# A part of the low-part subtractions goes from VectorE to GpSimd

## The chip, the cores and the metric

The kernel runs on one core of one Trainium2 chip. The metric is the device time of one execution in microseconds; the median of several executions is compared.

## The reference

The program takes one sequence of 256 tokens of width 1024, in float32, through two blocks of two layers each.

The first block has a hybrid layer (a gated linear recurrence with a short convolution beside retention), a feed-forward layer `(silu(x @ w1) * (x @ w3)) @ w2` with 2816 hidden columns, a sparse-attention layer (compressed, selected and windowed keys; at 256 tokens all four selection blocks are taken), and a second feed-forward layer, each behind an RMS norm and with a residual sum. The second block has two layers of four branches (full attention, windowed attention with a sink, a Fourier mix, a spatial gate), each with a gated merge; they work on the tokens and, in the first of them, on a context of 256 more tokens, and their norms are modulated by vectors made from two condition vectors and the matrices `w_ada`.

Nearly all the time goes into matrix products of the 256 tokens with weights of 1024 rows. The result has to hold float32 accuracy.

## The kernel before

TensorE multiplies in the type `float32r`. To keep accuracy, each operand is split into a high part (the value rounded to that type by a ScalarE copy) and a low part (the value less its high part), and each product is three matmuls: low by high, high by low, high by high (`mm3`, L420, L421, L422, the first operand being the stationary one).

Weights lie in three lists in memory, cut into pieces of 128 x 1024 in the order in which they are used: `wmain` (object `w_x`, all that the tokens' layers need), `wctx` (`w_c`, the context's projections) and `wada` (`w_a`, the modulation's matrices). A piece comes in through one of four `raw` buffers by a DMA on SyncE's queue (`load`, L316). `Weights.parts` then makes its two parts: ScalarE copies `raw` to the high part `whi` (L339), VectorE subtracts to get the low part `wlo` (L340), both into one of three pairs of buffers or into a big buffer with another name (M, B, C). The raw buffer is free for the next load when both have read it. `w_x` makes one piece ahead of the one asked for (`ahead` 1). `k` counts the pieces made. The list `los` holds the subtractions, and `behind` uses it to keep some VectorE instructions (L811 in the group norm, L1127 in the query and key norm) behind the next subtraction in VectorE's order.

The order of the instructions on each engine comes from the framework's scheduler, which works from the program's order, from what is ready by its own estimates, and from a few orders written out with `tc.issue_after`. Each engine then works through its instructions in order.

The stages that the change touches:

- The hybrid layer takes 32 pieces: four each for q, xr, k, v, g and y, eight for the output. Its group norm takes a power on GpSimd (L475) between VectorE instructions (L474, L811).
- The residual sum (L614) and the norm before the first feed-forward layer follow: squares on ScalarE, small VectorE instructions (L485, L486), a power on GpSimd (L487), a scaled copy on VectorE (L493), transposes on TensorE (L511).
- The first feed-forward layer (`ffn`) has 22 blocks. Block j takes two up pieces, applies the gate, and splits the result (tile `fp`); from block 2 on one down piece follows each time, for the block two before (`Out.step`). Before each block `hook(j)` runs: it moves the modulation on by two steps (`first`), and from block 8 on the context layer by two (`side_by`). A modulation step loads one piece of `wada` into a raw buffer and adds it, scaled, to two sums on VectorE (L1089 for the first, L1091 for the others); 18 steps make two modulation vectors, and so they end with block 8.
- The third stage (`nsa`) projects, then runs 16 units of attention; in each the context moves on by one step.

GpSimd does only powers of a few columns and some fills.

## Time and profile before

| | |
|---|---|
| median of three runs | 1454.93 us (1454.76 to 1458.89) |
| profiled execution | 1458.04 us, its span 1456.3 us |
| TensorE busy | 1402.7 us, 96% of the span |
| VectorE busy | 962.7 us, 66% |
| ScalarE busy | 710.2 us, 49% |
| GpSimd busy | 38.6 us, 3% |
| mean granted TensorE clock | 0.984 |

The span runs from the first to the last instruction of the profiled execution. Matmuls are pipelined and their ends are modelled, so that a busy TensorE is not TensorE at its peak. In the rows PE is TensorE, DVE is VectorE, ACT is ScalarE, POOL is GpSimd and SPq is SyncE's queue of DMA issues.

### The profile page before, as it was taken

How to read it: one execution, taken by the hardware profiler on the slowest of the kernel's cores; microseconds unless marked ns; L12 is line 12 of the kernel's file. 1: busy time of each engine (PE TensorE's matmuls, PEld its weight loads, DVE VectorE, ACT ScalarE, POOL GpSimd, SP SyncE). 2: the span in 40 equal slices, each digit the busy share in tenths (PEclk: the TensorE clock that was granted, in tenths of full speed). 3: DMA queues.
4: the chain of work that ended last, by engine and by line, in shares of the span. 5: the costliest groups of instructions: out<-in, count | busy, mean ns of one | idle time of the engine just before them, and what ended most of it. 6: DMA issues, size and time to landing. Idle time of an engine off the chain costs nothing.

```text
span 1456.3 us, 24385 instructions
## 1 busy us (share of the span) xinstructions
PE 1402.7 (96%) x9815; PEld 1265.0 (87%) x9815; DVE 962.7 (66%) x1675; ACT 710.2 (49%) x1203; POOL 38.6 (3%) x46
## 2 busy tenths in 40 slices
PE   7998999999899999999999999999999999999998
PEld 6887889988697678989888798999999878889997
DVE  7967886645676677768776776354443677665566
ACT  5743446456455664444445575333332345654453
POOL 0010000000000000000000100000000011100000
PEclk9999999999998999999999999999999999999999
DMA  8645777546353026677775553233333516413663
GB/s 295 210 126 189 259 254 234 181 138 196 97 151 117 1 63 211 212 238 231 229 259 178 155 159 89 72 117 103 116 117 116 159 64 184 151 53 109 187 181 124
DMA packets 65745, 230.31 MB, mean 158 GB/s; under 512 B 7776, under 2 KB 9312, under 8 KB 65376
## 3 DMA queue, kind: packets, MB, share of 16 engines
q1 hardware_dynamic: 65632, 228.76, 49.9%
q8 instruction: 77, 1.26, 0.4%
q14 instruction: 36, 0.29, 0.1%
HBM read 227.68 MB, written 1.05 MB: 157 GB/s over the span
## 4 chain that ended last, share of the span: by engine, by line
PE 76%; DVE 9%; DMA 6%; ACT 5%; issue 3%; POOL 1%; SPq 0%; ACTq 0%; DVEq 0%; POOLq 0%
PE P L420 12%; PE P L421 12%; PE P L422 12%; PE Q L420 6%; PE Q L422 6%; PE Q L421 6%; PE R L420 4%; PE R L421 4%; PE R L422 4%; DVE wlo L340 3%; DMA raw<-in_wmain_dram 3%; PE P L431 3%; DMA raw<-in_wada_dram 2%; PE R L428 2%; PE Q L431 2%
## 5 line engine op out<-in xcount | busy, mean ns | idle before, releaser
L340 DVE TENSOR_TENSOR wlo<-raw,whi 128x1024 fp32r<-128x1024 f32 (+2 forms) x325 | 392.1, 1209 | 195.7 <-ACT whi L339 194.1
L339 ACT ACTIVATE whi<-raw 128x1024 fp32r<-128x1024 f32 (+2 forms) x325 | 340.3, 1048 | 323.6 <-PE P L422 80.2
L420 PE MATMUL P<-B,wlo 128*128 128x256 f32 x752 | 216.2, 287 | 0.0
L422 PE MATMUL P<-B,whi 128*128 128x256 f32 x752 | 213.7, 284 | 0.0
L421 PE MATMUL P<-B,whi 128*128 128x256 f32 x752 | 213.4, 284 | 0.0
L420 PE MATMUL Q<-B,wlo 128*128 128x256 f32 x704 | 202.7, 288 | 3.4 <-DVE wlo L340 2.4
L422 PE MATMUL Q<-B,whi 128*128 128x256 f32 x704 | 200.6, 285 | 0.0
L421 PE MATMUL Q<-B,whi 128*128 128x256 f32 x704 | 200.2, 284 | 0.0
L420 PEld LDWEIGHTS P<-B,wlo 128*128 128x128 f32 x752 | 143.8, 191 | 3.0 <-issue 1.4
L421 PEld LDWEIGHTS P<-B,whi 128*128 128x128 f32 x752 | 143.8, 191 | 0.7 <-issue 0.3
L422 PEld LDWEIGHTS P<-B,whi 128*128 128x128 f32 x752 | 143.8, 191 | 0.4 <-issue 0.2
L420 PEld LDWEIGHTS Q<-B,wlo 128*128 128x128 f32 x704 | 135.9, 193 | 7.8 <-DVE wlo L340 4.0
L421 PEld LDWEIGHTS Q<-B,whi 128*128 128x128 f32 x704 | 136.0, 193 | 1.3
L422 PEld LDWEIGHTS Q<-B,whi 128*128 128x128 f32 x704 | 135.9, 193 | 0.3 <-issue 0.2
L420 PE MATMUL P<-whi,B 128*128 128x512 f32 (+3 forms) x264 | 101.4, 387 | 5.3 <-DVE B L411 5.3
L421 PE MATMUL P<-wlo,B 128*128 128x512 f32 (+3 forms) x264 | 99.0, 376 | 0.5 <-DVE wlo L340 0.5
L422 PE MATMUL P<-whi,B 128*128 128x512 f32 (+3 forms) x264 | 98.9, 375 | 0.0
L1091 DVE SCALAR_TENSOR_TENSOR M<-raw,silu_c,M 128x1024 f32<-128x1024 f32 x42 | 53.8, 1281 | 36.9 <-DMA raw<-in_wada_dram 36.8
L420 PE MATMUL R<-C,wlo 128*128 128x256 f32 x272 | 76.3, 280 | 0.0
L421 PE MATMUL R<-C,whi 128*128 128x256 f32 x272 | 76.0, 279 | 0.0
L422 PE MATMUL R<-C,whi 128*128 128x256 f32 x272 | 75.9, 279 | 0.0
L420 PE MATMUL P<-whi,fp 128*128 128x512 f32 x160 | 62.0, 409 | 4.8 <-ACT whi L339 4.8
(485 smaller groups left out, 2856.2 us busy)
## 6 DMA issues: line engine op xcount, KB each, us to landing
raw<-in_wmain_dram SPq DMA_DIRECT2D x324, 512.0 KB, 4.1
raw<-in_wada_dram SPq DMA_DIRECT2D x48, 512.0 KB, 4.4
raw<-in_wctx_dram SPq DMA_DIRECT2D x26, 512.0 KB, 3.9
raw<-in_wmain_dram SPq DMA_DIRECT2D x8, 384.0 KB, 3.1
F<-in_rows_dram SPq DMA_DIRECT2D x4, 512.0 KB, 5.1
C<-in_ctx_dram SPq DMA_DIRECT2D x2, 1024.0 KB, 5.0
C<-in_params_dram SPq DMA_DIRECT2D x3, 512.0 KB, 4.4
ring<-in_rows_dram SPq DMA_DIRECT2D x6, 256.0 KB, 5.3
```

The lines of the kernel that those rows point to most:

```text
L339: self.nc.scalar.activation(hi, src, AF.Copy)
L340: self.los.append(self.nc.vector.tensor_sub(lo, src, hi).ins)
L420: pe.matmul(o, l[1], r[0], start=first, stop=False)
L421: pe.matmul(o, l[0], r[1], start=False, stop=False)
L422: pe.matmul(o, l[0], r[0], start=False, stop=last)
L428: pe.matmul(o, l[a], r[b], start=k == 0, stop=k == 2)
L431: pe.matmul(o, l, r, start=first, stop=last)
L1091: dve.scalar_tensor_tensor(a, t, mods[nm][:, k:k + 1], a, OP.mult, OP.add)
```

## The change

`Weights` gets a number `share`, 0 at first. Where it is set, each piece whose count `k` is a multiple of it has its low part subtracted by GpSimd; such a subtraction isn't entered in `los`. `w_x.share` is 3 from the start of the hybrid layer and 0 from the tenth block (j = 9) of the first feed-forward layer on; `w_c.share` is 1 in the third stage and 0 before and after. The hook of the first feed-forward layer becomes a function of its own and otherwise does what it did.

```diff
         self.off = 0
         self.at = 0
+        self.share = 0
...
         self.nc.scalar.activation(hi, src, AF.Copy)
-        self.los.append(self.nc.vector.tensor_sub(lo, src, hi).ins)
+        if self.share and self.k % self.share == 0:
+            self.nc.gpsimd.tensor_sub(lo, src, hi)
+        else:
+            self.los.append(self.nc.vector.tensor_sub(lo, src, hi).ins)
         return hi, lo
...
+    w_x.share = 3
     o = run(hybrid(lambda: None))
...
     w_c.slots = ["M1", "M2", "M3"]
-    o = run(ffn(0, "C1", lambda j: (first(j, 0 if j < 0 else 2), side_by(0 if j < 8 else 2)), add(o)))
+    def ffn0_hook(j):
+        w_x.share = 3 if j < 9 else 0
+        first(j, 0 if j < 0 else 2)
+        side_by(0 if j < 8 else 2)
+
+    o = run(ffn(0, "C1", ffn0_hook, add(o)))
     run(m)
-    w_c.slots = []
+    w_c.slots, w_c.share = [], 1
     o = run(nsa(lambda p=None: side_by(0 if p is None or p < 0 else 1), add(o)))
+    w_c.share = 0
```

## Rows read from the trace of the kernel before

**Rows 1.** The page, parts 1 and 2: busy time, and TensorE's clock by slice.
```profile
PE 1402.7 (96%) x9815; PEld 1265.0 (87%) x9815; DVE 962.7 (66%) x1675; ACT 710.2 (49%) x1203; POOL 38.6 (3%) x46
...
PEclk9999999999998999999999999999999999999999
```

**Rows 2.** Busy time by stretch: us, then each engine's, clock, DMA share, GB/s.
```profile
25.00:60.00 35.00, 35.00 (x209) 30.93 (x208) 32.57 (x79) 23.64 (x39) 0.24 (x1) 1.00 0.74 245
...
119.00:135.00 16.00, 10.96 (x58) 8.99 (x57) 12.50 (x19) 6.05 (x12) 1.12 (x2) 0.86 0.45 136
135.00:217.00 82.00, 77.36 (x539) 71.06 (x538) 73.18 (x82) 33.80 (x44) 0.00 (x0) 0.99 0.78 256
217.00:245.00 28.00, 28.00 (x196) 26.08 (x195) 21.42 (x30) 17.99 (x29) 0.00 (x0) 1.00 0.73 236
425.00:550.00 125.00, 119.53 (x801) 92.16 (x801) 88.66 (x330) 76.26 (x223) 0.00 (x0) 0.93 0.26 78
```

**Rows 3.** VectorE's groups by form, 135 to 215 us: busy us, mean ns.
```profile
L340 DVE TENSOR_TENSOR wlo<-raw,whi 128x1024 fp32r<-128x1024 f32 x24 | 28.8, 1219 | 3.3 <-ACT whi L339 3.2
L1091 DVE SCALAR_TENSOR_TENSOR M<-raw,silu_cc,M 128x1024 f32<-128x1024 f32 x14 | 17.9, 1278 | 0.0
L1091 DVE SCALAR_TENSOR_TENSOR M<-raw,silu_c,M 128x1024 f32<-128x1024 f32 x13 | 16.6, 1279 | 2.1 <-DMA raw<-in_wada_dram 2.1
L411 DVE TENSOR_TENSOR fp<-ring,fp 128x256 fp32r<-128x256 f32 x9 | 3.8, 418 | 0.7 <-ACT fp L411 0.7
```

**Rows 4.** Who waited for whom, 135 to 217 us: us, times, longest.
```profile
ACT whi L339 <- DMA raw<-in_wmain_dram: 18.9, 15, 6.2
...
PE P L420 <- ACT whi L339: 3.8, 6, 0.9
```

**Rows 5.** The DMA queue's own waits, 0 to 250 us.
```profile
SPq L316 <- DVE wlo L340: 100.0, 47, 7.1
```

**Rows 6.** GpSimd's groups by form: busy us, mean ns of one.
```profile
L475 POOL TENSOR_TENSOR r<-v,ident 128x8 f32<-128x8 f32 x2 | 3.7, 1834 | 33.1 <-DVE v L474 33.1
...
L985 POOL MEMSET fp<- 128x1024 f32 x1 | 1.0, 957 | 0.0
```

**Rows 7.** GpSimd in order of time: start us, us of the instruction.
```profile
799.44 1.37 POOL L1554 TENSOR_TENSOR r<-v,ident 128x1 f32<-128x1 f32 x1
...
808.23 0.59 POOL L1554 TENSOR_TENSOR r<-v,ident 128x1 f32<-128x1 f32 x1
...
1195.22 1.47 POOL L487 TENSOR_TENSOR r<-v,ident 128x1 f32<-128x1 f32 x1 [8.33 <-DVE v L486]
```

**Rows 8.** VectorE in order of time, beside two of these.
```profile
799.16 1.23 DVE L340 TENSOR_TENSOR wlo<-raw,whi 128x1024 fp32r<-128x1024 f32 x1 [0.38 <-ACT whi L339]
800.30 0.88 DVE L492 TENSOR_SCALAR M<-ring,r 128x512 f32<-128x512 f32 x2
...
1195.06 1.21 DVE L340 TENSOR_TENSOR wlo<-raw,whi 128x1024 fp32r<-128x1024 f32 x1
```

**Rows 9.** VectorE, then TensorE, at the residual sum before the norm.
```profile
116.86 1.23 DVE L340 TENSOR_TENSOR wlo<-raw,whi 128x1024 fp32r<-128x1024 f32 x1 [1.65 <-ACT whi L339]
118.00 0.68 DVE L614 TENSOR_TENSOR x<-x,P 128x512 f32<-128x512 f32 x1
...
116.86 0.39 PE L422 MATMUL P<-M,M 128*128 128x512 f32 x1
```

**Rows 10.** TensorE in order of time: one down piece's first two uses.
```profile
160.40 1.20 PE L420 MATMUL P<-whi,fp 128*128 128x512 f32 x4 [0.83 <-ACT whi L339]
...
164.31 0.40 PE L421 MATMUL P<-wlo,fp 128*128 128x512 f32 x1
```

**Rows 11.** VectorE in order of time, third stage.
```profile
446.14 0.76 DVE L974 TENSOR_TENSOR ring<-R,T 128x256 f32<-128x256 f32 x2 [3.96 <-PE R L422]
```

**Rows 12.** TensorE in order of time, first pieces.
```profile
16.30 0.50 PE L421 MATMUL P<-wlo,B 128*128 128x512 f32 x1 [0.53 <-DVE wlo L340]
```

**Rows 13.** TensorE in order of time, the group norm's second half.
```profile
107.32 0.66 PE L815 MATMUL R<-ident,ring 128*128 128x128 f32 x4 [1.33 <-DVE ring L812]
```

## The prediction

> **What bounds the kernel now.** I read the page first. TensorE is busy for 96% of the span and its clock stands near full in every slice [rows 1], so a change off TensorE can pay only where TensorE waits. Then I cut the span into the stages that the change touches [rows 2]. Between 25 and 60 us TensorE is busy without a gap, although VectorE is at 32.57 of 35 us: there is nothing to win there, only something to lose. From 119 to 135 us, where the first feed-forward layer's norm runs, it is busy for 10.96 of 16 us. From 135 to 217 us, the first nine blocks of that layer, it is busy for 77.36 of 82 us, so 4.64 us are idle, and VectorE has 73.18 of 82 us of work: it is nearly full too. From 217 us, when the modulation is done, TensorE has no gap left and VectorE drops to 21.42 of 28 us. In the third stage's attention (425 to 550 us) TensorE misses 5.5 us, and VectorE is at 88.66 of 125 us.
>
> The waits between 135 and 217 us name the reason [rows 4]. TensorE waits 3.8 us in six pieces for the high part `whi` of a weight piece. ScalarE, which makes `whi`, waits 18.9 us for the raw piece to land. The queue's own waits say why the raw piece is late [rows 5]: in the first 250 us its loads waited 100.0 us, 47 times, for `wlo` subtractions on VectorE. Each load needs one of four raw buffers, and a buffer comes free only when VectorE has read it. So VectorE's order bounds this stage by way of the raw buffers. What VectorE does there is in [rows 3]: subtractions of 1.219 us, L1091 of 1.28 us, and small things.
>
> **The change part by part.** The counter `k` numbers the main pieces. The hybrid stage has 32 of them, so one in three puts pieces 3, 6 to 30 on GpSimd (10). The feed-forward layer begins with piece 33; blocks 0 and 1 have two pieces each and every later block two up pieces and one down piece, so 33, 36 and then exactly the down pieces 39, 42 to 57 go (9). By the time the tenth block begins, 58 pieces are made, one being made ahead. That is 19 in all. In the third stage the context makes two pieces just before and after 446 us, and perhaps two more late.
>
> *The price of one subtraction on GpSimd.* The trace of before has none. The nearest row is GpSimd's memset of 128x1024, 0.957 us, which writes once and reads nothing [rows 6]; the subtraction reads twice and writes once, so less than 0.96 us is excluded, and three such passes are 2.9 us. The other end is the power: 1.834 us for eight columns, 0.23 us a column, or 235 us for 1024. A power is a long computation for each element and the memset is not; a subtraction is nearest to the memset, so I take 2 to 2.9 us, 2.4 in the middle. By the far end 19 subtractions would take 4.5 ms; I give that under 1 in 50 and leave it out of the range.
>
> The Trainium skill (GPSIMD Engine Reference, Performance versus the Vector engine) has 4497 ns for a two-input add of 2048 columns; half of it, an estimate of 2.25 us, would make the sum 1.2 us smaller over eight subtractions and changes no case.
>
> *Is the longer subtraction itself hidden?* In the layer, yes. A down piece's `whi` starts four L420 matmuls at 160.40 us, as soon as it is made, and its `wlo` is first read at 164.31 [rows 10]. That is 3.9 us of cover for 2.4 us, and still enough if GpSimd first waits 1.2 us for a VectorE subtraction.
>
> *Does GpSimd work beside VectorE?* This decides the size, and the trace bears on it. GpSimd's power of one column takes 0.59 us when VectorE is not in its way. At 799.44 us it took 1.37 us: VectorE had begun a subtraction at 799.16 and its next instruction started at 800.30, and GpSimd finished 0.51 us after that [rows 7, 8]. At 1195.22 it took 1.47 us beside a VectorE subtraction that began at 1195.06. So an instruction of VectorE with two inputs in SBUF holds GpSimd back until it ends. Whether a long GpSimd read holds VectorE back as well no row shows: the powers read only a few columns.
>
> *Blocks 0 to 8.* VectorE instructions with two SBUF inputs fill 28.8 + 17.9 + 16.6 + 3.8 = 67.1 of the 80 us from 135 to 215 [rows 3]. The change takes eight subtractions away, 8 x 1.219 = 9.8 us, so 57.3 us stay and 22.7 us (28%) are free of them. GpSimd needs 8 x 2.4 = 19.2 us. If it falls on free time at that share, 0.7 us of each runs beside VectorE and 1.7 us are paid by one of the two. If VectorE pays, it loses 1.7 and gains 1.2 us for each piece, 8 x 0.5 = 4 us more, which its 82 - 73.18 = 8.8 us of idle can mostly take. If GpSimd pays, VectorE is 9.8 us lighter and the 4.6 us of TensorE waits can go, but the down piece's raw buffer is held longer. Bounds: -4.6 and +9.2 us (worked out under the slower rival). I take 0.
>
> *The norm.* Piece 33's subtraction stands at 116.86 us in front of the residual add L614, which starts at 118.00; the last matmul that the add needs began at 116.86 and ended at 117.25 [rows 9]. On GpSimd it frees 118.00 - 117.25 = 0.75 us on the path to the norm's transposes. It would end about 2.4 us after 116.9, near 119.3; the norm's power comes behind it on GpSimd. The two later subtractions there are pieces 34 and 35 and stay. I take -0.7; bounds -0.75 and +0.5, if the power has to queue.
>
> *The first 25 us.* TensorE waits 0.53 us at 16.30 for piece 2's subtraction [rows 12]; piece 3 comes next. On GpSimd it either leaves VectorE free sooner (-0.5) or, held against VectorE, stands in the way of piece 2 for most of the 2.4 - 1.2 = 1.2 us (+1.1). I take +0.3.
>
> *Hybrid stage after that.* Nine more subtractions. The wait that they add: the group norm's two powers are on GpSimd, queued behind pieces 24 and 27. Behind the second one stand L811 and L812 on VectorE, and then the transposes at 107.32 us, for which TensorE already waited 1.33 us [rows 13]. Also, L811 is held behind a subtraction in VectorE's list, and one on GpSimd is no longer in that list. Bounds -0.5 and +1.5; I take +0.3. Elsewhere VectorE's extra time is covered by pieces split ahead.
>
> *Third stage.* Behind the first context subtraction VectorE sat idle for 3.96 us before 446.14 anyway, waiting for TensorE [rows 11]; the second stands among softmax steps and can gain or lose its own length once. I take 0, bounds -1 and +1.
>
> Sum: 0 - 0.7 + 0.3 + 0.3 + 0 = -0.1 us. The profiled execution took 1458.04 us with a span of 1456.3, so 1.7 us lie around the span; it is 3.1 us above the median of the runs shown, 1454.93. Put on that median the change gives 1454.8 us.
>
> **The rivals.** *Faster: VectorE is relieved and GpSimd costs it nothing.* For it: VectorE is nearly full exactly where TensorE waits, and its releases set the loads. Against it: the blocked powers. The time: -4.6 in the blocks, -0.75 at the norm, -0.5 at the start, -5.8 us, 1449.1.
>
> *Slower: a GpSimd subtraction holds VectorE off.* The place is blocks 0 to 8: if nothing of GpSimd's 2.4 us runs beside VectorE, each piece costs it 2.4 - 1.2 = 1.2 us, 8 x 1.2 = 9.6 us; if half of VectorE's 8.8 us of idle takes part of this, 9.6 - 4.4 = 5.2 us reach TensorE (with a subtraction of 2.9 us, 8 x 1.7 - 4.4 = 9.2). With +1.1 at the start, +1 at the group norm and -0.7 at the norm it is +6.6 us, 1461.5. It decides when more than 1.2 us of each subtraction is time in which VectorE stands still. For it: such instructions fill 67 of 80 us and one direction of the blocking is in the rows. Against it: the other direction is in none.
>
> The Trainium skill (SBUF — State Buffer, Who interferes with whom) says that a VectorE instruction with two SBUF inputs contends with a GpSimd instruction that reads SBUF. By that rule this rival is what happens; the trace agrees for the one direction that it shows (1.37 us in place of 0.59).
>
> *The change does little of what it says:* GpSimd takes the pieces, but the loads stay as late, since the down piece's buffer is released as late as before; this ends at the forecast's time.
>
> **How the numbers follow.** About 0.3%, 4.4 us, is what a measurement of this kernel can tell from no change. No change in that sense, with the costs and gains above nearly balanced and the loads as late as before: 0.40, with 1450.6 to 1459.3 as its own range. The faster rival beyond the bound: 0.33. The slower one: 0.27. The range reaches to both rivals, 1448 to 1463: it leaves out a gain beyond all waits named here, and of the slower side the part above a subtraction of some 2.6 us.
>
> **What would show it.** L340 on GpSimd, 19 times and two to four more in the third stage, 2 to 2.9 us where nothing blocks it; 8 subtractions fewer on VectorE from 135 to 217 us; L614 near 117.3 us. VectorE's L340 or L1091 of over 1.3 us, or idle time released by GpSimd, speaks for the slower rival; ScalarE's wait for raw pieces well under 18.9 us and TensorE idle for less than 2 us there for the faster. The forecast is wrong if the order of the instructions shifts elsewhere, for example so that TensorE's clock falls in another place.

## The result, and the profile after

The changed kernel takes 1477.47 us in the median (1472.37 to 1478.98), against 1456.33 us of the kernel before in the same session: ratio 1.0133, 95% interval 1.0112 to 1.0154. It is 21 us slower where 0.1 us less was forecast, and lies above the range. The profiled execution took 1476.06 us, its span 1474.3.

L316 and L339 are now L318 and L341; later lines move by five: L340 is L345 on VectorE and L343 on GpSimd, L420 to L422 are L425 to L427, L614 is L619, L811, L812 and L815 are L816, L817 and L820, L1091 is L1096.

TensorE's busy time, from the page of the kernel after, answers to [rows 1]. It is 5.8 us longer, in a span that is 18.0 us longer: two thirds of the loss are waiting, and the rest is the same matmuls taking longer.

```profile
PE 1408.5 (96%) x9815; PEld 1270.8 (86%) x9815; DVE 963.9 (65%) x1654; ACT 709.3 (48%) x1203; POOL 95.5 (6%) x67
```

VectorE ran 21 instructions fewer and was busy for 1.2 us longer. The stages of [rows 2] in the kernel after, the windows moved with the work:

```profile
25.00:60.00 35.00, 32.71 (x197) 29.00 (x196) 34.20 (x68) 21.64 (x35) 12.75 (x4) 1.00 0.71 225
129.00:145.00 16.00, 11.50 (x61) 9.64 (x60) 13.09 (x19) 5.62 (x11) 1.11 (x2) 0.84 0.50 146
145.00:236.00 91.00, 80.20 (x537) 73.34 (x536) 72.29 (x75) 33.79 (x44) 21.20 (x8) 0.95 0.69 229
444.00:569.00 125.00, 119.35 (x801) 92.21 (x800) 86.83 (x327) 76.25 (x222) 4.71 (x2) 0.93 0.26 79
```

In the hybrid stage TensorE, which had no gap, now misses 2.29 of 35 us. The nine blocks take 91 us for 82. TensorE idles for 10.8 us there in place of 4.64, 6.2 us more; and its mean granted clock is 0.95 in place of 0.99, which is 0.05 x 91 - 0.01 x 82 = 3.7 us more of lost full speed. Together these are the 9 us, within the rounding of the clock.

VectorE's largest group in these blocks, to be read against [rows 3]: the subtractions are 17 for 24, but one takes 1520 ns for 1219.

```profile
L345 DVE TENSOR_TENSOR wlo<-raw,whi 128x1024 fp32r<-128x1024 f32 x17 | 25.8, 1520 | 5.1 <-ACT whi L341 5.1
```

The waits of the blocks, beside [rows 4], and the DMA queue's waits from 0 to 250 us, beside [rows 5]: ScalarE waits for the raw pieces as before, TensorE waits for low parts, and the loads wait for GpSimd where they waited for VectorE.

```profile
ACT whi L341 <- DMA raw<-in_wmain_dram: 21.3, 13, 6.5
...
PE P L426 <- POOL wlo L343: 4.2, 2, 2.5
PE Q L425 <- DVE wlo L345: 3.8, 2, 2.4
```

```profile
SPq L318 <- DVE wlo L345: 64.5, 22, 7.4
SPq L318 <- POOL wlo L343: 50.0, 18, 4.1
```

GpSimd's groups give what [rows 6] could not, the price of a subtraction:

```profile
L343 POOL TENSOR_TENSOR wlo<-raw,whi 128x1024 fp32r<-128x1024 f32 x19 | 52.1, 2743 | 136.2 <-ACT whi L341 136.2
...
L343 POOL TENSOR_TENSOR M<-raw,M 128x1024 fp32r<-128x1024 f32 x2 | 4.7, 2357 | 16.5 <-ACT M L341 16.5
```

Undisturbed it is 2.36 us (the context's two); the 19 others have a mean of 2.74 and a longest of 5.49. The forecast's 2.4 was right.

**Where the 21 us arise.** The next table compares the start of the same instruction in two profiles, the kernel named less the kernel before, in us. The columns stand at these times of the kernel before: 32 a ScalarE copy of xr, 57 the copy behind TensorE's transposes of `M`, 91 the first gelu, 115 and 126 the first and last residual sum L614, 154 and 211 the silu of blocks 3 and 9, 365 the first residual sum after the layer, 549 that after the third stage.

```
kernel                        32    57    91   115   126   154   211   365   549
after                       +1.7  +3.6  +5.0 +10.3  +9.5 +14.1 +18.8 +19.2 +18.9
hybrid alone                +1.6  +3.3  +5.7  +9.4  +8.7  +8.6  +8.2  +8.3  +5.5
feed-forward alone          -0.2  -0.2  -0.2  -0.2  -0.9  +3.3  +7.8  +7.9  +4.2
extra subtractions          +1.3  +5.4 +10.2 +11.8 +13.6 +16.3 +20.5 +20.4 +14.6
extra fills                 +0.9  +1.0  +6.0  +8.2  +8.0  +9.9  +9.6  +9.5  +5.0
extra copies                +1.0  +1.3  +2.3  +2.6  +2.4  +3.7  +3.3  +3.2  -2.3
narrow subtractions         +2.3  +3.9  +4.8 +10.4 +10.2 +21.5 +42.8 +42.8 +42.1
third stage alone           +0.9  +0.9  +0.9  +0.9  +0.9  +1.7  +2.5  +3.3  +2.0
feed-forward, other third   +0.9  +0.9  +0.9  +0.8  +0.2  +2.5  +6.1  +6.5  +0.8
hybrid, beside chains       +0.8  +1.9  +3.2  +6.0  +6.4  +6.1  +6.8  +6.7  +2.4
hybrid, other pieces        +2.4  +3.2  +3.2  +3.5  +4.4  +4.4  +7.3  +7.4  +4.9
hybrid, chains twice        +1.7  +2.9  +8.5 +15.0 +15.2 +16.6 +17.8 +17.7 +14.7
hybrid, others twice        +4.8 +13.1 +13.1 +18.1 +16.9 +19.5 +21.8 +21.9 +18.4
third stage twice           +0.1  +0.1  +0.1  +0.1  +0.6  +2.9  +2.0  +2.0  +2.8
norm's piece alone          +1.4  +1.4  +1.4  +1.3  +0.8  +1.3  +2.9  +2.8  -3.3
fills in place              +1.1  +1.0  -0.7  +0.3  +0.4  +0.5  +0.6  +0.5  -1.2
```

How far one profile may be trusted can be seen in it too. From 32 to 115 us the five kernels that don't change the hybrid stage agree with the kernel before within 0.1 us. At the start the kernels that don't touch it scatter from -0.2 to +1.7; from 126 to 211 us, in unchanged blocks, from -0.5 to +4.9; from 365 to 549 us, in an unchanged third stage, from -6.1 to -2.5.

A second measure comes from the spans and mean granted clocks of all runs: (1 - clock) x span is what the clock took away, if TensorE was busy all the time. The next table has, in us, the mean time of a kernel's runs less that of the kernel before in the same session, the part of it that is lost clock, and the rest, mostly waiting. The parts are good to about 1 us, and to 2 us for kernels with four to six runs.

```
kernel                     time  clock   rest
hybrid alone              +12.2   +6.4   +5.8
feed-forward alone         +9.0   +6.4   +2.7
feed-forward, other third  +2.1   -0.9   +3.1
extra subtractions        +18.6   +6.9  +11.7
extra fills                +9.9   +6.8   +3.0
extra copies               +3.7   +1.3   +2.5
narrow subtractions       +43.9  +19.0  +24.9
hybrid, beside chains      +5.9   +1.8   +4.1
hybrid, other pieces       +4.6   +0.6   +4.0
hybrid, chains twice      +15.7   +6.6   +9.1
hybrid, others twice      +15.0   +5.5   +9.6
third stage alone          +2.2   +2.4   -0.3
third stage twice          +2.6   +3.3   -0.7
norm's piece alone         +0.2   +0.2   -0.0
fills in place             +1.1   +2.5   -1.5
```

**How VectorE is held.** GpSimd in order of time, then VectorE, then TensorE, in the kernel after:

```profile
26.16 2.40 POOL L343 TENSOR_TENSOR wlo<-raw,whi 128x1024 fp32r<-128x1024 f32 x1 [9.29 <-ACT whi L341]
...
43.17 5.49 POOL L343 TENSOR_TENSOR wlo<-raw,whi 128x1024 fp32r<-128x1024 f32 x1 [5.57 <-ACT whi L341]
56.47 2.36 POOL L343 TENSOR_TENSOR wlo<-raw,whi 128x1024 fp32r<-128x1024 f32 x1 [7.81 <-ACT whi L341]
...
107.94 2.34 POOL L343 TENSOR_TENSOR wlo<-raw,whi 128x1024 fp32r<-128x1024 f32 x1
```

```profile
26.30 2.29 DVE L679 TENSOR_SCALAR lam<-lam 128x4 f32<-128x4 f32 x1
28.61 0.17 DVE L678 TENSOR_TENSOR lam<-lam,lam 128x4 f32<-128x4 f32 x1
...
46.34 2.60 DVE L744 SCALAR_TENSOR_TENSOR C<-C,C 128x256 f32<-128x256 f32 x1
...
56.93 2.45 DVE L637 TENSOR_TENSOR M<-ring 128x512 f32<-128x512 f32 x1
...
108.00 2.83 DVE L816 TENSOR_TENSOR ring<-ring,r 128x512 f32<-128x512 f32 x1 [1.54 <-POOL r L480]
```

```profile
59.52 0.63 PE L709 MATMUL R<-ident,M 128*128 128x128 f32 x4 [2.29 <-DVE M L637]
...
111.60 0.66 PE L820 MATMUL R<-ident,ring 128*128 128x128 f32 x4 [3.46 <-DVE ring L817]
```

Four columns on VectorE take 2.29 us at 26.30 and 0.17 at 28.61. The first began behind a GpSimd subtraction and ended 0.03 us after it. At 46.34 a VectorE instruction of 256 columns ends 0.28 us after the GpSimd subtraction beside it, at 56.93 and 108.00 those of 512 columns 0.55 us after it, as if they did their own work only then. Over the first 600 us fifteen VectorE instructions take over 0.1 us longer than the median of their kind in the kernel before, 24 us in all (holds are counted so from here on): what a VectorE instruction is charged here is the rest of the GpSimd instruction that was running, not a share of its own length. At 43.17 it goes the other way as well: GpSimd takes 5.49 us, because VectorE was first. The TensorE rows say where it matters: the product at 56.93 and the ring sum behind 108.00 are links of serial chains, and TensorE waits 2.29 and 3.46 us behind them (nothing and 1.33 us before, [rows 13]).

The Trainium skill (SBUF — State Buffer, Who interferes with whom) says that whoever is first holds the shared ports for its whole instruction; these rows agree, down to the 0.03 us at 28.6. It adds that VectorE instructions with two inputs in SBUF meet GpSimd instructions that read, and not fills; in the runs with fills below no such instruction is held. Two inputs are not the only condition: the instruction at 26.30 reads one tensor, and so do the few that fills held, by 0.7 us at most.

### The profile page after: what moved, and what is told of

It is laid out like the page before. It is cut to its first block, busy times and chain, and to the rows that moved or that the text cites. A ratio compares the mean times of both kernels' runs of the same rounds, so it can differ in the third digit from the quotient of the medians.

```text
span 1474.3 us, 24381 instructions
## 1 busy us (share of the span) xinstructions
PE 1408.5 (96%) x9815; PEld 1270.8 (86%) x9815; DVE 963.9 (65%) x1654; ACT 709.3 (48%) x1203; POOL 95.5 (6%) x67
## 4 chain that ended last, share of the span: by engine, by line
PE 74%; DVE 9%; DMA 6%; ACT 5%; issue 3%; POOL 1%; SPq 0%; ACTq 0%; DVEq 0%; POOLq 0%
PE P L425 12%; PE P L426 12%; PE P L427 12%; PE Q L425 5%; PE Q L426 5%; PE Q L427 5%; PE R L426 4%; PE R L425 4%; PE R L427 4%; DVE wlo L345 3%; DMA raw<-in_wada_dram 3%; PE P L436 3%; DMA raw<-in_wmain_dram 2%; DVE M L1096 2%; PE R L433 2%
## 5 line engine op out<-in xcount | busy, mean ns | idle before, releaser
L345 DVE TENSOR_TENSOR wlo<-raw,whi 128x1024 fp32r<-128x1024 f32 (+2 forms) x306 | 375.8, 1230 | 197.9 <-ACT whi L341 196.5
L341 ACT ACTIVATE whi<-raw 128x1024 fp32r<-128x1024 f32 (+2 forms) x325 | 340.2, 1048 | 323.9 <-issue 78.8
L425 PE MATMUL P<-B,wlo 128*128 128x256 f32 x752 | 216.2, 288 | 0.0
L427 PE MATMUL P<-B,whi 128*128 128x256 f32 x752 | 213.8, 284 | 0.0
L425 PE MATMUL Q<-B,wlo 128*128 128x256 f32 x704 | 204.5, 291 | 5.3 <-DVE wlo L345 4.4
L427 PE MATMUL Q<-B,whi 128*128 128x256 f32 x704 | 202.6, 288 | 0.0
L426 PE MATMUL Q<-B,whi 128*128 128x256 f32 x704 | 202.4, 287 | 0.0
L425 PEld LDWEIGHTS P<-B,wlo 128*128 128x128 f32 x752 | 143.8, 191 | 3.0 <-issue 1.2
L425 PEld LDWEIGHTS Q<-B,wlo 128*128 128x128 f32 x704 | 137.8, 196 | 8.9 <-DVE wlo L345 5.7
L427 PEld LDWEIGHTS P<-B,whi 128*128 128x128 f32 x752 | 143.8, 191 | 0.4 <-issue 0.2
L426 PEld LDWEIGHTS Q<-B,whi 128*128 128x128 f32 x704 | 138.0, 196 | 1.4
L427 PEld LDWEIGHTS Q<-B,whi 128*128 128x128 f32 x704 | 138.0, 196 | 0.3 <-issue 0.2
L425 PE MATMUL P<-whi,B 128*128 128x512 f32 (+3 forms) x264 | 101.9, 388 | 4.6 <-DVE B L416 4.6
L427 PE MATMUL P<-whi,B 128*128 128x512 f32 (+3 forms) x264 | 98.9, 375 | 0.0
L1096 DVE SCALAR_TENSOR_TENSOR M<-raw,silu_c,M 128x1024 f32<-128x1024 f32 x42 | 54.0, 1285 | 38.2 <-DMA raw<-in_wada_dram 38.1
L425 PE MATMUL R<-C,wlo 128*128 128x256 f32 x272 | 76.3, 281 | 0.0
L427 PE MATMUL R<-C,whi 128*128 128x256 f32 x272 | 76.0, 280 | 0.0
L426 PE MATMUL P<-wlo,fp 128*128 128x512 f32 x160 | 64.1, 401 | 4.2 <-POOL wlo L343 4.2
```

The costliest lines, as they stand in the source:

```text
L341: self.nc.scalar.activation(hi, src, AF.Copy)
L345: self.los.append(self.nc.vector.tensor_sub(lo, src, hi).ins)
L425: pe.matmul(o, l[1], r[0], start=first, stop=False)
L426: pe.matmul(o, l[0], r[1], start=False, stop=False)
L427: pe.matmul(o, l[0], r[0], start=False, stop=last)
L1096: dve.scalar_tensor_tensor(a, t, mods[nm][:, k:k + 1], a, OP.mult, OP.add)
```

## The experiments

**One stage alone.** In the first kernel `w_x.share` is 3 in the hybrid layer only, in the second in the feed-forward layer only; the third stage is as before in both.

```diff
 hybrid alone
-        w_x.share = 3 if j < 9 else 0
+        w_x.share = 0
 feed-forward alone
-    w_x.share = 3
     o = run(hybrid(lambda: None))
 both
-    w_c.slots, w_c.share = [], 1
+    w_c.slots = []
```

> Only pieces 3, 6 to 30 of the hybrid layer on GpSimd, nothing in the feed-forward layer and in the third stage. Theory 1 (a GpSimd subtraction holds VectorE off, and VectorE's late instructions hold TensorE up, wherever the subtraction falls): by the shift of the residual add in the two profiles (114.5 to 124.8 us) this part alone costs 8 to 11 us. Theory 2 (the loss comes from the down pieces of the feed-forward layer alone, whose low part comes late): 0 to 2 us.

Measured: 1467.68 us, ratio 1.0075 (1.005 to 1.0101). The mark near 115 us is at +9.4. Of the 7.8 us between 32 and 115 us, some 4.6 are idle time of TensorE and 3.4 lost clock; the waits behind the two links above grow by 4.3 us.

> Only pieces 33 to 57, of the first feed-forward layer. Theory 1: the other half, 8 to 11 us, so that the two parts add up to the whole. Theory 2: the whole loss, 17 to 20 us.

Measured: 1462.97 us, ratio 1.0063 (1.0041 to 1.0085). The norm moves forward by 0.7 us and the blocks lose 8.7. The two losses add up: 0.75% + 0.63% = 1.38%, against 1.33% for the whole. More than half of the loss is in the stage that the forecast had put at +0.6.

**The hold without the dependence.** All low parts stay on VectorE, and the third stage is as before. At the same 19 pieces GpSimd works on a scratch tile of 340 columns that nobody reads: three subtractions, or three copies, or seven fills behind a copy of one column.

```diff
+        if self.share and self.k % self.share == 0:
+            for c in (0, 340, 680):
+                self.nc.gpsimd.tensor_sub(self.scr, hi[:, c:c + 340], self.scr)
 fills, in the place of the loop
+            self.nc.gpsimd.tensor_copy(self.scr[:, :1], hi[:, :1])
+            for n in (340,) * 7:
+                self.nc.gpsimd.memset(self.scr[:, :n], 0.0)
 copies, in the loop
+                self.nc.gpsimd.tensor_copy(self.scr, hi[:, c:c + 340])
```

> All low parts stay on VectorE, and at the same 19 pieces GpSimd makes, for nobody, three more subtractions of 340 columns from the piece's high part into a scratch buffer; no instruction waits for their result. Theory 1: VectorE is held off all the same and not relieved, so the kernel is slower by 12 to 25 us, and VectorE's short instructions take up to 1 us more beside them. Theory 3 (the low part comes later from GpSimd, 2.4 in place of 1.2 us, and TensorE waits for that; the engines do not disturb each other): within 2 us of the kernel before.

Measured: 1472.92 us, ratio 1.0119 (1.0093 to 1.0145). Nobody waits for GpSimd's results here and VectorE has its old work, and yet nine tenths of the loss are there. Not all of it need be the hold: two powers of the norms also queue behind the new work on GpSimd, for 1.3 and 0.9 us. GpSimd's and VectorE's rows, in order of time:

```profile
25.82 4.90 POOL L345 TENSOR_TENSOR scr<-whi,scr 128x340 f32<-128x340 f32 x3 [8.85 <-ACT whi L341]
```

```profile
26.85 0.88 DVE L675 TENSOR_TENSOR lam<-lam 128x4 f32<-128x4 f32 x1
```

An instruction of 0.16 us takes 0.88: the hold is now 0.7 us, most of one subtraction of 340 columns. There are 39 holds of 24 us in all, as much as the fifteen long ones in the kernel after.

> As the run before, but GpSimd reads only one column of the high part and then fills the scratch buffer seven times (some 2.4 us of writing, no reading). Theory 1 in the form that reading is what holds VectorE off: within 3 us of the kernel before. In the form that any GpSimd work on SBUF holds it off: slower by 12 us or more, as with the subtractions.

Measured: 1463.71 us, ratio 1.0063 (1.0038 to 1.0087), with 0.5 us of holds in all. That is in neither range. The loss lies elsewhere: the mark at 65 us is at +1.0 and the one at 91 at +6.0. GpSimd, then TensorE, in that stretch:

```profile
64.29 2.93 POOL L344 COPY scr<-whi 128x1 f32<-128x1 f32 x1 [3.00 <-ACT whi L341]
67.28 3.01 POOL L346 MEMSET scr<- 128x340 f32 x7
70.26 0.55 POOL L493 TENSOR_TENSOR r<-v,ident 128x1 f32<-128x1 f32 x1
```

```profile
74.48 2.79 PE L437 MATMUL Q<-M,ring 128*128 128x64 f32 x12 [2.20 <-DVE ring L786]
```

The copy of one column took 2.93 us, held by two VectorE subtractions; the norm's power (L493 here) had to queue behind it and the seven fills; VectorE's scaled copy waited 2.51 us for the power, and TensorE 2.20 us for what follows. Its clock was full until then, and from 70 to 80 us its mean granted clock is 0.72: the twelve matmuls at 74.48 take 2.79 us, and the same twelve take 1.45 us at 82.79, at full speed. So a second cost of work on GpSimd is its own queue, with powers in it that a chain waits for. The kernel after doesn't pay it: its powers from 60 to 250 us start 0.08 us after their operand, as before. This control was not as clean as intended, since the copy of one column reads.

> All low parts stay on VectorE. At the same 19 pieces GpSimd copies three times 340 columns of the piece's high part into a scratch tile that nobody reads: the run with three extra subtractions (1472.92 us, 23 us of holds on VectorE) with an operation of one tensor operand in the place of one with two. If VectorE is held off by GpSimd instructions with two tensor operands and not by others, the holds fall under 3 us and the time comes to that of the run with fills, 1460 to 1466 us. If any GpSimd instruction that reads SBUF holds VectorE, the holds stay at 15 us or more and the time at 1469 us or more.

Measured: 1460.52 us, ratio 1.0021 (1.0003 to 1.004). GpSimd's group, and one VectorE row:

```profile
L345 POOL COPY scr<-whi 128x340 f32<-128x340 f32 x57 | 65.6, 1151 | 119.5 <-ACT whi L341 117.2
```

```profile
56.13 0.95 DVE L637 TENSOR_TENSOR M<-ring 128x512 f32<-128x512 f32 x1
```

The time is in the first range of the expectation; the holds are in neither: 25, 5.7 us in all, none over 0.31 us. The product that lost 1.77 us in the kernel after loses 0.27. A read of one operand holds VectorE too; it only ends sooner. The other half is on GpSimd's side: the copies have a mean of 1.15 us, for they wait for VectorE's.

**Shorter instructions.** The changed kernel, with each GpSimd subtraction cut into eight.

```diff
-            self.nc.gpsimd.tensor_sub(lo, src, hi)
+            for c in range(0, w, 128):
+                self.nc.gpsimd.tensor_sub(lo[:, c:c + 128], src[:, c:c + 128], hi[:, c:c + 128])
```

> The change with each GpSimd subtraction of 1024 columns cut into eight of 128. If a VectorE instruction is held off for as long as the one GpSimd instruction that is running lasts (2.0 to 3.4 us in the changed kernel, 0.6 to 0.7 us beside subtractions of 340 columns), no single hold is longer than about 0.4 us: the tiny instructions of the norms lose under 0.4 us in place of 2 us, the sum of the holds falls from 24 us to under 12 us, and the time comes to 1460 to 1468 us. If the hold belongs to the tile, or is paid in full whatever the width, the sum stays at 20 us or more and the time at 1472 us or more. Should VectorE and GpSimd take turns instruction by instruction, each GpSimd subtraction of a tile takes longer than 2.4 us, up to 5 us, and whoever waits for it loses that.

Measured: 1499.32 us, ratio 1.0294 (1.0269 to 1.0319), the slowest of all. GpSimd's group, GpSimd and VectorE in order of time, and TensorE's wait from 135 to 250 us:

```profile
L344 POOL TENSOR_TENSOR wlo<-raw,whi 128x128 fp32r<-128x128 f32 x152 | 101.0, 700 | 118.6 <-ACT whi L341 118.6
```

```profile
229.15 7.75 POOL L344 TENSOR_TENSOR wlo<-raw,whi 128x128 fp32r<-128x128 f32 x8 [6.31 <-ACT whi L341]
```

```profile
229.66 2.88 DVE L346 TENSOR_TENSOR wlo<-raw,whi 128x1024 fp32r<-128x1024 f32 x2
...
233.59 1.60 DVE L1097 SCALAR_TENSOR_TENSOR M<-raw,silu_c,M 128x1024 f32<-128x1024 f32 x1 [1.06 <-DMA raw<-in_wada_dram]
```

```profile
PE P L427 <- POOL wlo L344: 16.1, 7, 3.4
```

The first part of the theory holds: no VectorE instruction is held for much over 0.3 us. The holds sum to 13.5 us for 24, a little over the 12 that were expected. The last sentence of the expectation decides the time: the engines take turns, and each eighth waits for a VectorE instruction of 1.3 us. One piece takes up to 7.75 us, and TensorE waits 16.1 us for low parts in the blocks. The long instruction was the milder choice.

**Which piece is moved in the blocks.** Feed-forward alone, the piece shifted by one, so that an up piece goes to GpSimd and not the down piece.

```diff
-        if self.share and self.k % self.share == 0:
+        if self.share and self.k % self.share == 1:
```

> The run that changed the feed-forward layer alone (1462.97 us), with the piece that GpSimd takes moved by one: a piece of the gate and up projection in each block in place of the down projection's. The order of the first down projection's matmuls on TensorE is then again as before. If the loss in the blocks (+8.6 us from the norm to block 8 in that run) is VectorE held off by the GpSimd subtraction, it stays: 1460 us or more, holds of 6 to 12 us. If it is that the low part of the down piece is now needed right behind its high part, so that the GpSimd subtraction's 2.4 us lie open, it goes: 1454 to 1457 us.

Measured: 1458.82 us, ratio 1.0012 (0.9997 to 1.0028), with six holds, 8.3 us in all, as many as the down pieces gave (seven, 8.1 us). That is between the two expectations: the holds are those of the first, and the ratio is nearer to the second. GpSimd, VectorE and TensorE:

```profile
142.33 2.34 POOL L343 TENSOR_TENSOR wlo<-raw,whi 128x1024 fp32r<-128x1024 f32 x1 [12.51 <-ACT whi L341]
```

```profile
142.47 3.28 DVE L345 TENSOR_TENSOR wlo<-raw,whi 128x1024 fp32r<-128x1024 f32 x1
```

```profile
144.72 0.39 PE L425 MATMUL Q<-B,wlo 128*128 128x256 f32 x1 [2.07 <-POOL wlo L343]
```

So the time is 7 us better than with the down pieces, but the waits are not. In this profile TensorE waits 5.8 us for VectorE's low parts in the blocks and 2.1 for GpSimd's, with the down pieces 3.9 and 3.8, before 0.6 and nothing. The rest in the table of the runs is alike too, +3.1 and +2.7 us; the 7 us are lost clock, -0.9 against +6.4. Why more clock is lost with the down pieces wasn't found. How a down piece's low part comes late: the kernel after, block 2's down piece, on GpSimd, VectorE and TensorE:

```profile
159.68 3.64 POOL L343 TENSOR_TENSOR wlo<-raw,whi 128x1024 fp32r<-128x1024 f32 x1 [8.70 <-ACT whi L341]
```

```profile
159.91 1.22 DVE L345 TENSOR_TENSOR wlo<-raw,whi 128x1024 fp32r<-128x1024 f32 x1
161.87 2.54 DVE L345 TENSOR_TENSOR wlo<-raw,whi 128x1024 fp32r<-128x1024 f32 x1 [0.74 <-ACT whi L341]
```

```profile
159.66 1.20 PE L425 MATMUL P<-whi,fp 128*128 128x512 f32 x4 [1.59 <-ACT whi L341]
163.38 0.50 PE L426 MATMUL P<-wlo,fp 128*128 128x512 f32 x1 [2.52 <-POOL wlo L343]
...
164.07 0.41 PE L425 MATMUL Q<-B,wlo 128*128 128x256 f32 x1
```

The first low part is used right behind the four high parts, and only then come the up piece's matmuls (from 164.07). Before they stood between the two, as they do for the next block's down piece in [rows 10]. The scheduler, given a low part that is no longer in VectorE's list, ordered TensorE's work anew here. GpSimd began at 159.68, waited for VectorE's subtraction at 159.91, and ended at 163.32; TensorE stood for 2.52 us, after 1.59 for the high part. Behind this gap the granted clock is at half, 1.2 GHz, from 163.8 to 167.2 us: matmuls of 0.41 us, where those of the same size at 155 us take 0.28. It takes both, the order and the late low part. The last kernel below, in which GpSimd fills the low part, has the same order on TensorE, and there the same piece waits for no low part:

```profile
149.08 1.20 PE L425 MATMUL P<-whi,fp 128*128 128x512 f32 x4 [0.40 <-ACT whi L341]
150.12 0.39 PE L426 MATMUL P<-wlo,fp 128*128 128x512 f32 x1
```

The other wait for GpSimd in the blocks, 1.71 us at 226.72, is of this sort as well.

**Which pieces of the hybrid stage.** Hybrid alone, with only the four pieces that lay beside chains, or only the six others.

```diff
-        if self.share and self.k % self.share == 0:
+        if self.share and self.k in (15, 18, 24, 27):
 the counterpart
+        if self.share and self.k in (3, 6, 9, 12, 21, 30):
```

> Of the ten low parts of the hybrid stage, GpSimd takes only the four (the 15th, 18th, 24th and 27th piece) whose subtractions ran beside one link of a serial chain in the run that changed the hybrid stage alone: the query product at 56.6 us, the norm factor at 69.1, the group mean at 93.7 and the ring sum at 109.1. If the loss of that run (+8 to +9 us at the end of the stage) comes from those links, each held 1.8 to 2.1 us with TensorE waiting behind it, most of it stays: +5 us or more at the sum with the residual near 115 us, 1460 us or more. If every subtraction costs about alike because VectorE is the fullest engine there (34 of 37 us busy from 25 to 62 us), four of ten leave +3 to +4 us, 1457.5 to 1459 us.

> The counterpart: GpSimd takes the other six low parts of the hybrid stage (the 3rd, 6th, 9th, 12th, 21st and 30th piece). If the links of the chains set the loss, +3 us or less remains near 115 us, the most of it at the start (+1.7 us at the first rotation), 1455 to 1458.5 us. If every subtraction costs alike, +5 to +6 us, 1459.5 to 1462 us.

Measured: 1462.61 us, ratio 1.0035 (1.0015 to 1.0056) for the four, and 1461.81 us, 1.003 (1.0013 to 1.0046) for the six: alike, within the intervals. The four came out as the links would have it, the six by the time as if every subtraction cost alike. TensorE's waits for VectorE from 30 to 119 us, first of the four, then of the six:

```profile
PE R L820 <- DVE ring L817: 4.2, 2, 2.7
...
PE R L709 <- DVE M L637: 1.5, 1, 1.5
```

```profile
PE R L820 <- DVE ring L817: 2.1, 2, 1.3
...
PE R L709 <- DVE M L637: 0.7, 1, 0.7
```

The kernel before has 2.1 us of the first wait and none of the second, so the four add 3.6 us and the six 0.7. From 32 to 115 us, where profiles repeat, the four lose 5.2 us and the six 1.1, with holds of 7.8 and 5.1 us there (7.8 and 8.3 in the whole stage). The six lose at the ends of the stage: they start it at +2.4 and lose another 0.9 from 115 to 126. To tell links of chains from VectorE's load as a whole, each group was run once more with the suspected cost doubled, each low part being subtracted twice; and so was the third stage (below).

```diff
             self.nc.gpsimd.tensor_sub(lo, src, hi)
+            self.nc.gpsimd.tensor_sub(lo, src, hi)
```

> The run with the four hybrid pieces beside chains, each low part subtracted twice by GpSimd, the second time with the same result; TensorE's, VectorE's and ScalarE's orders are those of that run. If links of chains that wait for GpSimd set the loss, a second subtraction behind each doubles what a link can lose: +8 us or more near 115 us (+6.0 with one) and 1464 us or more. If the cost of a piece is that VectorE as a whole has less time, 5 us or less is added to either group and the four cost less than the six.

> The counterpart with the six other pieces, twelve GpSimd subtractions in place of six. If only links of chains matter, it stays within 3 us of the single run, 1459 to 1463 us, +3 to +6 us near 115 us. If every subtraction costs alike, six pieces with two each lose half as much again as the four with two each: 1467 us or more where the four are at 1464.

Measured: 1471.7 us, ratio 1.011 (1.0091 to 1.0128) for the four, and 1469.87 us, 1.01 (1.0078 to 1.0121) for the six. TensorE's longest wait that is new from 30 to 121 us, first of the four, then of the six:

```profile
PE P L427 <- POOL wlo L344: 2.7, 1, 2.7
```

```profile
PE P L426 <- DVE wlo L346: 4.7, 1, 4.7
```

The four did what doubling should, to 15 us near 115 us; the six, which were to stay within 3 us of the single run, went beyond it too. So it is not the links alone. One GpSimd subtraction beside a chain costs 0.35% x 1456 / 4 = 1.3 us, one of the others 0.7; the intervals overlap. Doubled, 1.011 gives 16 us for eight, 2.0 each (1.7 to 2.3), and the others cost 1.2 (0.9 to 1.5), so a place beside a chain does cost more. From 32 to 115 us the others are nearly covered as long as VectorE is late by one hold; with two it is late enough that an ordinary low part comes 4.7 us after TensorE wants it (32 to 57 us, +4.8 to +13.1).

**The norm's piece, and the third stage.** The kernel named in the next expectation was meant to hold both, but no piece is made between the two calls of the hook, so only the third stage's two subtractions moved. The norm's piece was then run alone.

```diff
 both
-    w_x.share = 3
 third stage alone
-        w_x.share = 3 if j < 9 else 0
+        w_x.share = 3 if j < 0 else 0
 norm's piece alone (third stage as before)
-        w_x.share = 3 if j < 9 else 0
+        w_x.share = 3 if j == 0 else 0
```

> GpSimd takes the one low part that VectorE worked on at the start of the feed-forward layer's norm, and the context's in the third stage; hybrid and the nine blocks are as before. The norm's chain then starts 0.7 to 1.1 us earlier, as in the run that changed the feed-forward layer alone (-0.8 to -1.2 us there), and the later marks keep it: 1452.9 to 1453.9 us against 1454 us before, ratio 0.9992, which the rounds can't tell from no change but the marks of the profile can. If the loss in the third stage is larger than 0.3 us, the marks after it show it.

Measured: 1457.93 us, ratio 1.0014 (0.9999 to 1.0028), some 2 us at most.

> The third stage alone, each of the context's two low parts subtracted twice. The profiles with a changed third stage come out of it 0.3 to 1.7 us earlier than they went in, against the kernel before, those with an unchanged one 2.5 to 6.1 us, so the change there may cost 2 to 3 us, by the hold on VectorE or by the order of TensorE's instructions, of which 19 differ in all of them. If it is the hold, the doubled subtraction adds 2 us or more: 1460 us or more. If it is the order, the time is that of the single run, ratio 1.0005 to 1.0025.

Measured: 1458.12 us, ratio 1.0018 (1.0004 to 1.0032), no more than with one subtraction, although GpSimd works twice as long. The holds there are 2.0 us in the profile with one subtraction and 0.9 with two, so the doubling didn't double them; but the time doesn't follow them either. So a hold is not what costs these 2 us, if they are there. Five profiles have the two pieces moved, one of them with fills and no hold; from 365 to 549 us their marks change by -1.7 to +0.8, those of the eleven others by -6.1 to -2.5. That difference is lost clock: 8.5 to 10.2 us of this stretch in the five, 3.4 to 6.8 in the eleven. The kernel before, with an unchanged stage, lost 10.2 as well, so profiles don't settle it; the table of the runs puts the 2 us down to the clock too (+2.4 and +3.3, the rest -0.3 and -0.7). It would fit the few instructions of TensorE near 457 us whose order the change alters there; a run with that order and VectorE's subtraction wasn't tried.

> GpSimd takes one low part only, the one on which VectorE worked at 116.9 us at the start of the feed-forward layer's norm. If VectorE being free there is what moved the norm forward in the run that changed the feed-forward layer alone (-0.7 us from the mark near 115 us to the one near 118), the same step appears here and stays to the third stage: the mark near 118 us lies 0.6 to 1.2 us earlier against the mark near 115, and the median is 0.5 to 1.2 us under that of before, too little for the rounds. If the GpSimd subtraction costs something there too, by a hold on the norm's small instructions (0.16 us each, held up to 2.1 us), the step is zero or a loss of up to 2 us.

Measured: 1456.74 us, ratio 1.0001 (0.9987 to 1.0014). From the mark at 115 us to that at 126 the norm moves forward by 0.5 us (in feed-forward alone by 0.7). But in hybrid alone, where VectorE keeps the norm's piece, it is 0.7 us too, so the gain isn't shown, and no median shows it.

**The relief alone.** The change, with GpSimd filling the low part with zeros in the place of subtracting.

```diff
-            self.nc.gpsimd.tensor_sub(lo, src, hi)
+            self.nc.gpsimd.memset(lo.bitcast(FT), 0.0)
```

> The change with GpSimd filling the low part with zeros in place of subtracting, at the same 19 pieces and the two of the context: the low part of these pieces is left out of the computation. VectorE is relieved of the same 21 subtractions, the fills (0.96 us each, no tensor operand) do not hold it, and the low part is there before the high part. So this is what the relief of VectorE alone is worth. If the change loses only by what GpSimd's reading instructions cost, the time falls below that of before: -0.7 us at the feed-forward norm for certain, and up to -4 us where VectorE is 34 of 37 us busy in the hybrid stage, 1450 to 1455 us. If VectorE's load was never on the path there, it is 1454 to 1457 us, no different from before. If it is slower than before by over 4 us, the loss of the change has another source than the hold: the order of the program that goes with the moved piece, or the powers queued behind GpSimd's work.

Measured: 1457.01 us, ratio 1.0007 (0.9994 to 1.002). Its windows, in the hybrid stage and in the nine blocks:

```profile
25.00:62.00 37.00, 37.00 (x218) 32.71 (x217) 30.66 (x78) 25.33 (x41) 3.50 (x5) 1.00 0.72 246
...
135.00:217.00 82.00, 77.42 (x539) 70.54 (x538) 64.37 (x73) 33.84 (x44) 7.64 (x8) 0.99 0.74 255
```

VectorE is 8.8 us lighter in the blocks than in [rows 2] (64.37 for 73.18), and TensorE's busy time is the same, 77.42 for 77.36. One hold (0.7 us), no loss, and no gain that the interval shows. The table of the runs has 1.5 us less waiting against 2.5 us more lost clock, so the relief may save some 1.5 us of waiting, which the time doesn't show.

This run also takes away a rival. Its instructions stand in exactly the order of the changed kernel on TensorE, VectorE and ScalarE through the hybrid stage, the norm and the first down piece. Near 115 us the changed kernel is at +10.3 us, this one at +0.3. So the new order of the instructions, which came with the change, costs nothing there by itself; GpSimd's subtractions do.

## Why the prediction was wrong

**The hybrid stage** is the step that failed most. It said "Bounds -0.5 and +1.5; I take +0.3. Elsewhere VectorE's extra time is covered by pieces split ahead"; the start had +0.3. Measured for the stage alone: 0.75%, 11 us, of which 7.8 lie between 32 and 115 us. The wait that it named, powers queued on GpSimd, didn't come. Pieces split ahead do nearly cover a subtraction that is one hold late (the six others, 1.1 us); they don't cover a late link of a chain (the four, 5.2 us), nor two holds. Half of the loss with this stage alone is lost clock (6.4 of 12.2 us), which has no term in the sum. The forecast priced the hold only against VectorE's subtractions and only in the blocks, whereas here it falls on whatever comes next: four columns of a parameter, or the sum that TensorE waits for. The windows had said that TensorE has no gap there, that VectorE is at 32.57 of 35 us, and that there was only something to lose; the sum did not follow them. The start itself (+1.7, with up to +1.7 in kernels that don't change it) can't be told from +0.3.

**The blocks** were put at 0 and gave 0.63%, 9 us, for other reasons than the ones weighed. The holds, 8.1 us, are under half of the 19 us that GpSimd's eight subtractions were to take, and VectorE's busy time did not grow (72.29 us, before 73.18), so its load as a whole is not the cost. What failed is "3.9 us of cover for 2.4 us, and still enough if GpSimd first waits 1.2 us". The wait of 1.2 us came (3.64 us at 159.68). Where TensorE kept its order the cover held; in block 2 and at 226.72 the change itself had altered that order. These two waits are half of the new ones, and VectorE's own low parts, late by a hold, the other half. By the table of the runs the waits are some 3 of the 9 us; 6 are lost clock.

**The slower rival** had the right mechanism and the wrong place: GpSimd's reads do hold VectorE. It was priced at +6.6 us. The run with extra subtractions shows it without the late low parts, and without the relief: 1.19%, 17 us, with two queued powers among them. The missing term in it is TensorE's clock: around the new gaps at 111.60 (3.46 us) and 163.38 (2.52 us) the granted clock is at half from 112.6 to 116.0 and from 163.8 to 167.2 us, a further 1.7 us each; not behind all of them, as from 62 to 72 us, after the 2.29 us at 59.52, it is 1.00. The prediction named the clock only in its last sentence and gave it no price.

**The faster rival** is excluded by the last experiment. That VectorE's order bounds the loads was inferred from 100.0 us of queue waits [rows 5]. With a third of the subtractions gone ScalarE still waited 16.9 us for raw pieces (18.9 in [rows 4]) and TensorE's gaps stayed. But the loads also still waited 85.6 us for the subtractions that VectorE kept. So the reading isn't refuted; it is the inference from it, that a third fewer would bring the pieces sooner, that failed. What would bring them sooner wasn't tried.

**Right:** the price of a subtraction (2.36 us undisturbed) and the counts, 19 and two. The norm's -0.7 agrees with the marks (-0.5 to -0.8), but these can't be put down to the move. The third stage, put at 0 with bounds of 1 us, costs 2 us by the medians; the interval of one kernel with only this stage changed reaches down to 0, that of the other to 0.6 us.

## What to carry to other kernels

Before work goes to GpSimd, list the VectorE instructions that may run beside it, the small links of serial chains first, and charge each with up to the whole GpSimd instruction; whether VectorE has idle time on average doesn't answer it. Count the clock as well: a new gap on TensorE can cost its own length and, behind it, half of a stretch at half speed (1.7 us each, twice in the kernel after). Then ask what the relief is worth with the expensive part left out, as the fills did here: 1.0007 (at the least 0.9994) says that there was hardly anything to win before the price of the move came up. A cover read from the order before holds only as long as the order does, so moving an operation to another engine needs its consumers' order looked at again.

## What the runs showed of the hardware

The hold is by instruction and in both directions. Beside subtractions of 1024 columns VectorE lost up to 2.2 us at a time, beside 340 columns 0.7 to 0.8, beside 128 columns about 0.3; beside fills almost nothing (0.5 us over 133 of them). GpSimd's own instructions grew in turn, from 2.36 to 5.49 us at the longest, and a copy of one column to 2.93. Cutting the work finer moved the loss from VectorE to GpSimd and made the kernel slower again, 1.0294 for 1.0133.

An unchanged stage can differ by several us between two profiles. The third stage of the kernel before, then that of the kernel with the norm's piece alone, of which nothing in that stage is changed (columns as in [rows 2]):

```profile
365.00:549.00 184.00, 174.53 (x1097) 139.46 (x1096) 127.40 (x409) 105.09 (x270) 4.33 (x6) 0.94 0.30 88
```

```profile
368.10:545.90 177.80, 168.35 (x1096) 133.83 (x1095) 126.88 (x410) 104.09 (x270) 4.32 (x6) 0.98 0.29 92
```

The window is moved with the work. TensorE idles alike in both, 9.47 and 9.45 us; the whole difference of 6.2 us is its busy time, at a granted clock of 0.94 and 0.98. The lost full speed, 0.06 x 184 = 11 us and 0.02 x 178 = 4 us, covers it. That is the size of the scatter of single runs of the kernel before (1450.94 to 1462.91 us), and why steps of 1 us were read from marks and not from medians.
